# S5's B, C and tap matrices computed where they are used, from power tables transposed once

## The chip, the cores and the metric

One core of a Trainium2 chip runs the kernel. The metric is the device time of one execution in microseconds (us). TensorE is PE, VectorE DVE, ScalarE ACT, GpSimd POOL; SyncE (SP) issues all DMAs.

## The reference

Two layers, width 2048, over one sequence of 256 tokens. Each layer normalises x, multiplies it by one input matrix `w_in`, feeds the columns to four MoBA heads, four NSA heads and an S5 block (1024 channels in 64 groups of 16, each with 64 complex states), gates the three branches with SiLU and multiplies them by `w_out`. What the change touches is S5:

```python
mag = jnp.exp(dt * ar); ang = dt * ai
abar_r, abar_i = mag * jnp.cos(ang), mag * jnp.sin(ang)
nr, ni = abar_r - 1.0, abar_i
den = ar * ar + ai * ai
fr = (nr * ar + ni * ai) / den; fi = (ni * ar - nr * ai) / den
bbar_r = fr[..., None] * br - fi[..., None] * bim
bbar_i = fr[..., None] * bim + fi[..., None] * br
bu = einsum('bsgc,gpc->sbgp', ug, bbar)          # complex
x_t = abar * x_{t-1} + bu_t                      # associative scan
y = Re(einsum('sbgp,gcp->bsgc', x, c)) + d * u
```

## The kernel before, in words

**Projections.** Weights come in pieces of 512 KB: two rows of 128 inputs by 512 columns (`raw`). ACT rounds a piece to `whi`, DVE computes the remainder `wlo`; this pair is called a split here. Activations have the same two halves, `lhs`. PE then makes 12 products of 512 columns: `whi` with both halves and `wlo` with the high one. There are four buffers for `raw` and four for the halves of the weights. The columns of a layer come in chunks of 8 pieces, the first two (S5's inputs) together as 16 pieces named k=0 to 15 here; then the GLU and `wo`.

**S5.** `s5_setup` computes on [128, 64] tables the powers 0 to 4 of abar (`pwr`, `pwi`), f (`fr`, `fi`) and the phase `f4`. `s5_tables` loads B and C of half a layer (`bc`) and multiplies B by f in place. `s5_turns` lays scaled B out as `bpl` (ACT copies of 64 partitions) and makes the cosine and sine tables of the scan. A layer has 8 groups (`s5_group`), each with G=4 pairs of channel groups: `products` multiplies B by four powers (`PB`), PE transposes the four 128x128 blocks of `PB` into a PSUM bank, ACT copies the bank to `W1`; `products` multiplies C by three powers, ACT copies in power 0 and gathers all of it into `Cs`. Then PE forms the tap matrices from `Cs` and `bpl` (`w<-Cs,bpl`), multiplies, DVE scans, and PE multiplies the scan's result by C.

**Order.** Python generators (`Weave`) say after which weight piece a step may come, by the delays in `D`; the `Recorder` keeps every operation back, and `schedule` then lists them for all engines by priority, with estimated costs. PE's operations other than projection products are put into bursts between products; banks of PSUM are given out in order. `high_priority(offset)` moves an operation ahead by so many positions. All operations are issued on one line of a helper (L332, after the change L339), so tiles, not lines, tell them apart.

Of the kernel before, what the change touches and what calls it, by code (L numbers as in the profile page):

```python
# [29 lines left out]
G = 4  # L30
D = dict(sh=(1, 0), s0=(15, 21), s1=(4, 3), s2=(3, 5), s3=(1, 1), hn=(8, 4), hk=(4, 9), co=(8, 13), cg=(12, 5), cx=(3, 2), cp=(2, 2), at=(3, 8), pt=(2, 4), gap=(1, 2), ag=(3, 1), gt=(3, 4), lt=(1, 3), yt=(8, 4), gl=(0, 2), xt=(0, 45))
# [10 lines left out]
NEAR = 1  # L42
# [38 lines left out]
class Recorder:  # L81
# [24 lines left out]
    @staticmethod  # L106
    def box(ap):

        name = ap.tensor.name
        if name.startswith("in_") or name.startswith("out_"):  # L110
# [83 lines left out]
    def schedule(self):  # L194
# [67 lines left out]
        while left:  # L262
# [100 lines left out]
class Trunk:  # L363
# [62 lines left out]
    def load_consts(self):  # L426
        nc = self.nc
        t = self.cp.tile(list(self.a["cst"].shape), F, name="cst")
        nc.sync.dma_start(t, self.a["cst"])
        o = 0  # L430
        for nm, shape in cst_parts(self.L):
            n = math.prod(shape)
            v = t[:, o:o + n]
            if len(shape) > 1:
                v = v.rearrange(f"p ({' '.join('abc'[:len(shape)])}) -> p {' '.join('abc'[:len(shape)])}",
                                **dict(zip("abc", shape)))
            setattr(self, nm, v)
            o += n
        for nm, x in (("mask", self.mask), ("cmask", self.cmask), ("identb", self.ident)):
# [131 lines left out]
    def s5_setup(self):  # L571
# [5 lines left out]
        ar, ai, ld = self.a_re, self.a_im, self.logdt  # L577
# [25 lines left out]
        pr = self.cp.tile([128, n, 5], F, name="pwr")  # L603
        pi = self.cp.tile([128, n, 5], F, name="pwi")
        self.pr, self.pi = pr, pi
# [13 lines left out]
        self.rr = self.cp.tile([128, n, 4], F, name="pwrr")  # L619
        self.ri = self.cp.tile([128, n, 4], F, name="pwri")  # L620
        for q in range(4):
            nc.vector.tensor_copy(self.rr[:, :, q], pr[:, :, 4 - q])
            nc.vector.tensor_copy(self.ri[:, :, q], pi[:, :, 4 - q])
# [9 lines left out]
        self.fr = self.cp.tile([128, n], F, name="fr")  # L633
        self.fi = self.cp.tile([128, n], F, name="fi")
# [3 lines left out]
        tt(self.fr, t1, iv, OP.mult)  # L638
# [3 lines left out]
        tt(self.fi, t1, iv, OP.mult)  # L642
# [13 lines left out]
    def s5_tables(self, l, half):  # L656
        nc, sp, tt, ts = self.nc, self.sp, self.tt, self.ts
        n0 = 32 * l + 16 * half
        self.bc = sp.tile([128, 16, 4, 16], F, name="bc")
        nc.sync.dma_start(self.bc, self.a["bc"][l, :, 16 * half:16 * half + 16])  # L660
        br, bi = self.bc[:, :, 0], self.bc[:, :, 1]
        bb = lambda x: x[:, n0:n0 + 16, None].to_broadcast([128, 16, 16])
        t = [sp.tile([128, 16, 16], F, name=f"bt{j}", tag="g2", bufs=4) for j in range(4)]
        tt(t[0], br, bb(self.fr), OP.mult)
        tt(t[1], bi, bb(self.fi), OP.mult)
        tt(t[2], bi, bb(self.fr), OP.mult)
        tt(t[3], br, bb(self.fi), OP.mult)
        tt(br, t[0], t[1], OP.add)
        tt(bi, t[2], t[3], OP.subtract)

    def s5_turns(self, l, half):
        sp, tt = self.sp, self.tt
        n0 = 32 * l + 16 * half
        for h in range(2):
            q = slice(64 * h, 64 * h + 64)
            for r in range(2):
                self.act(self.bpl[64 * r:64 * r + 64, :, h, 16 * h:16 * h + 16], self.bc[q, :, r], AF.Copy)
# [11 lines left out]
    def s5_stream(self, l):  # L689

        if l == 0:
            yield from self.s5_setup()
# [5 lines left out]
        next(gens[0])  # L698
# [3 lines left out]
        for i in range(n + 2):  # L702
# [13 lines left out]
            if i < n:  # L716
                next(gens[i])
                if i + 1 < n:
                    if i + 1 == h:
                        self.s5_tables(l, 1)  # L720
                    next(gens[i + 1])
                if i % h == 0:
                    while not has(f"su{i // h}"):
                        yield 1
                next(gens[i])
                yield D["s1"][l] + (D["sh"][l] if i == h else 0)

    def s5_group(self, l, g):
# [4 lines left out]
        bc = self.bc[:, h0:h0 + G].rearrange("p a (t r) c -> p a t (r c)", t=2)  # L733

        def products(x, tr, ti, K, conj, first, **k):
            b = x[:, :, None, :].to_broadcast([128, G, K - first, 32])
            w = lambda v: v[:, n0:n0 + G, first:K, None].to_broadcast([128, G, K - first, 32])
            P = [sp.tile([128, G, K, 2, 16], F, **kw) for kw in (k, dict(name="P1", tag="g2", bufs=4))]
            for p, t in zip(P, (tr, ti)):
                tt(p[:, :, first:].rearrange("p a k r c -> p a k (r c)"), b, w(t), OP.mult)  # L740
            re, im = P[0][:, :, first:, 0], P[0][:, :, first:, 1]
            x0, x1 = (P[1][:, :, first:, q] for q in range(2))
            tt(re, re, x1, OP.add)
            tt(im, *((x0, im) if conj else (im, x0)), OP.subtract)
            return P[0]

        B = products(bc[:, :, 0], self.rr, self.ri, 4, False, 0, name="PB")
        yield
        W1 = sp.tile([128, G, 128], F, name="W1")
        pt = self.bank()  # L750
# [4 lines left out]
        for r in range(2):  # L755
            self.act(C[:, :, 0, r], bc[:, :, 1, 16 * r:16 * r + 16], AF.Copy, scale=1.0 - 2 * r)
        Cs = sp.tile([128, G, 2, 4, 16], F, name="Cs", bufs=2)
        for r in range(2):
            for e in range(2):
                self.act(Cs[64 * r:64 * r + 64, :, e], C[64 * e:64 * e + 64, :, :, r], AF.Copy)  # L760
# [607 lines left out]
    def run(self):  # L1368
        self.xd = self.dp.tile([128, 2, D_MODEL], F, name="xd")
        lhs = [None] * 16  # L1370
        with self.tc.high_priority(offset=40000):
# [8 lines left out]
            self.act(z, z, AF.Copy)  # L1380
        with self.tc.high_priority(offset=19000):
            self.nc.sync.dma_start(self.nw, self.a["nw"])
            self.load_consts()
# [38 lines left out]
def cst_parts(L):  # L1422
    return [("a_re", [L * 32]), ("a_im", [L * 32]), ("logdt", [L * 32]), ("dcol", [L, 32 // G]), ("jt", [64]),
            ("eye32", [32]), ("ident", [128]), ("ropec", [2, 32]), ("ropes", [2, 2, 16]), ("ropekc", [32]),
            ("ropeks", [2, 16]), ("valid", [2]), ("sel", [16]), ("mask", [128]), ("cmask", [2, 128]), ("mri", [2])]


def layout(inputs):
# [26 lines left out]
    d["a_re"], d["a_im"] = st(i["s5_a_re"]), st(i["s5_a_im"])  # L1455
    d["logdt"] = st(np.repeat(i["s5_log_dt"][:, :, None], 64, 2))
    b = lambda x: x.reshape(L, 32, 2, 64, 16).transpose(0, 2, 3, 1, 4).reshape(L, 128, 32, 16)
    g = lambda x: x.reshape(L, 32, 2, 16, 64).transpose(0, 2, 4, 1, 3).reshape(L, 128, 32, 16)
    d["bc"] = c(np.stack([b(i["s5_b_re"]), b(i["s5_b_im"]), g(i["s5_c_re"]), g(i["s5_c_im"])], 3))
# [20 lines left out]
```

## Time and profile before

| | |
|---|---|
| time, median of 3 runs | 869.31 us (869.24 to 869.38) |
| the profiled execution | 869.47 us |
| its span on the core | 867.7 us |
| busy: PE, PE weight load, DVE, ACT | 861.3, 710.0, 657.9, 568.4 us |
| bytes moved by DMA | 167.95 MB, 194 GB/s |
| TensorE clock granted | full in all 40 slices |

Busy time of an engine is the time in which an operation of it was under way. Operations of PE overlap in their records, so the step from one start to the next is what a product costs, and the recorded duration is longer.

### The profile page before, as it was taken

The page shows a single profiled execution, that of the slowest core. Times are in us where ns is not written, and L with a number is a line of the kernel's source. Part 1 is how long each engine was busy: PE and PEld are TensorE (multiplying, and loading weights), DVE is VectorE, ACT ScalarE, POOL GpSimd, SP SyncE. Part 2 cuts the span into 40 slices and gives each one's busy share as a digit, 9 for nine tenths or more (in the row PEclk, how much of TensorE's full clock was granted, in tenths as well). Part 3 has the DMA queues.
Part 4 walks back from the last instruction along what each step waited for, and adds up shares of the span by engine and source line. Part 5 has one row for each costly group of instructions (what it writes and reads, how often), then busy time and mean ns, then how long its engine had stood idle before and what let it go on. Part 6 is the DMA issues. An engine that isn't in the chain of part 4 may idle for free.

```text
span 867.7 us, 14290 instructions
## 1 busy us (share of the span) xinstructions
PE 861.3 (99%) x5107; PEld 710.0 (82%) x5107; DVE 657.9 (76%) x1381; ACT 568.4 (66%) x1084; POOL 10.3 (1%) x50
## 2 busy tenths in 40 slices
PE   9999999999999999999999999999999999999998
PEld 6888987877788888888888888888878888888886
DVE  6789999989868568755666899998996654675552
ACT  6588767687887866544645665697788575554331
POOL 1000000000000000000000000000000000000000
PEclk9999999999999999999999999999999999999999
DMA  9897486645524557677764666756552645665772
GB/s 310 279 297 232 132 282 208 205 126 178 157 65 138 184 170 243 194 243 242 225 213 132 197 215 205 252 176 194 168 171 74 205 130 161 188 191 182 242 242 97
DMA packets 66103, 167.95 MB, mean 194 GB/s; under 512 B 13424, under 2 KB 22128, under 8 KB 66032
## 3 DMA queue, kind: packets, MB, share of 16 engines
q1 hardware_dynamic: 66032, 167.04, 61.0%
q8 instruction: 40, 0.66, 0.3%
q14 instruction: 31, 0.25, 0.1%
HBM read 161.77 MB, written 5.24 MB: 192 GB/s over the span
## 4 chain that ended last, share of the span: by engine, by line
PE 84%; DVE 11%; DMA 2%; issue 1%; ACT 1%; SPq 0%; DVEq 0%; ACTq 0%
PE acc L332 72%; PE w L332 9%; DVE wlo L332 3%; PE o L332 3%; DVE t L332 1%; DMA raw<-in_w_a 1%; DVE Z L332 1%; DVE P L332 1%; ACT whi L332 1%; DVE q L332 1%; DMA raw<-in_w_p 1%; DVE z L332 1%; DVE qn L332 1%; DVE PB L332 0%; DVE XP L332 0%
## 5 line engine op out<-in xcount | busy, mean ns | idle before, releaser
L332 PE MATMUL acc<-whi,lhs 128*128 128x512 f32 (+1 forms) x2176 | 667.1, 386 | 0.1
L332 PEld LDWEIGHTS acc<-whi,lhs 128*128 128x128 f32 x2176 | 403.4, 188 | 82.2 <-issue 2.4
L332 DVE TENSOR_TENSOR wlo<-raw,whi 128x1024 fp32r<-128x1024 f32 (+2 forms) x275 | 323.7, 1179 | 163.7 <-ACT whi L332 162.7
L332 PE MATMUL acc<-wlo,lhs 128*128 128x512 f32 (+1 forms) x1088 | 418.0, 384 | 0.0
L332 ACT ACTIVATE whi<-raw 128x1024 fp32r<-128x1024 f32 (+2 forms) x275 | 281.5, 1026 | 191.5 <-PE acc L332 131.1
L332 PEld LDWEIGHTS acc<-wlo,lhs 128*128 128x128 f32 x1088 | 204.6, 188 | 40.4 <-issue 1.0
L332 ACT ACTIVATE P<-w,sst,hrs 128x128 f32<-128x128 f32 (+2 forms) x64 | 29.7, 477 | 8.0 <-DVE sst L332 7.7
L332 ACT ACTIVATE Cs<-P 64x256 f32<-64x256 f32 x64 | 26.5, 414 | 5.8 <-DVE P L332 2.6
L332 DVE TENSOR_TENSOR Z<-q,q 64x252 f32<-64x252 f32 x64 | 26.5, 414 | 0.9
L332 ACT ACTIVATE Uz<-Ud,cst 128x512 f32<-128x512 f32 x32 | 22.8, 719 | 4.5 <-DVE hrs_t L332 1.9
L332 ACT ACTIVATE sq<-acc,rstd 128x128 f32<-128x128 f32 x56 | 20.6, 368 | 5.0 <-DVE qn L332 4.1
L332 ACT ACT_TABLE_LOAD x14 | 18.0, 1283 | 3.0 <-DVE sst L332 2.1
L332 DVE TENSOR_TENSOR_SCAN z<-dec,t 128x512 f32<-128x512 f32 x16 | 19.3, 1206 | 0.1
L332 ACT ACTIVATE dec<-m 128x256 f32<-128x256 f32 x32 | 12.2, 410 | 8.7 <-DVE z L332 8.2
L332 PE MATMUL w<-Uz,W 128*64 128x128 f32 x256 | 17.5, 279 | 0.0
L332 DVE TENSOR_REDUCE sst<-w 128x2 f32<-128x512 f32 (+2 forms) x22 | 12.9, 599 | 5.2 <-PE w L332 5.2
L332 DVE TENSOR_TENSOR xc<-acc,xc 128x512 f32<-128x512 f32 x16 | 10.3, 683 | 7.9 <-PE acc L332 7.9
L332 DVE TENSOR_TENSOR lhs<-w,lhs 128x256 fp32r<-128x256 f32 x32 | 12.2, 416 | 4.5 <-ACT lhs L332 3.2
L332 PEld LDWEIGHTS w<-Uz,W 128*64 128x64 f32 x256 | 13.6, 136 | 1.5
L332 DVE SCALAR_TENSOR_TENSOR zs<-zt,zs 128x512 f32<-128x512 f32 x16 | 10.8, 686 | 4.0 <-ACT zs L332 4.0
L332 ACT ACTIVATE zt<-acc,rstd 128x512 f32<-128x512 f32 x16 | 11.0, 685 | 4.2 <-PE acc L332 4.0
L332 DVE STREAM_TRANSPOSE Ud<-su 128x256 f32<-128x256 f32 x32 | 13.6, 429 | 0.0
(234 smaller groups left out, 791.9 us busy)
## 6 DMA issues: line engine op xcount, KB each, us to landing
raw<-in_w_a SPq DMA_DIRECT2D x160, 512.0 KB, 4.5
raw<-in_wo SPq DMA_DIRECT2D x64, 512.0 KB, 4.7
craw<-in_cw SPq DMA_DIRECT2D x32, 256.0 KB, 3.6
raw<-in_glu SPq DMA_DIRECT2D x16, 512.0 KB, 4.2
raw<-in_w_p SPq DMA_DIRECT2D x15, 512.0 KB, 5.2
raw<-in_w_b SPq DMA_DIRECT2D x16, 268.0 KB, 4.0
xs<-in_x SPq DMA_DIRECT2D x8, 256.0 KB, 5.6
bc<-in_bc SPq DMA_DIRECT2D x4, 512.0 KB, 5.8
```

The costliest lines, as they stand in the source:

```text
L332: o.fn(*o.args, **o.kw)
```

## The change: what it does

`s5_setup` gets its three inputs (`sm`) in a DMA of their own behind k=2 and runs with a high priority from the beginning of the kernel. It ends with products of f and the powers (`tx`), four transposes of `tx` on PE, two ACT copies and eight DMAs to a DRAM table `tw`, and with sixteen ACT copies of 64 partitions into the tables `tc` and `tf`. Per group, `W1` is two loaded tables times two loaded copies of B (tables `T` read from `tw`, each row to 16 partitions; `B` laid out by the host): three operations of 512 columns on DVE, no transpose, no ACT copy. `Cs` is likewise three operations on DVE from `cc`, which the host lays out, and `tc`. `bpl` is two products and two sums on DVE. The smaller constants move: the masks have their own DMA, the rest comes later. The scheduler lets no more than four accumulator banks be out, and two delays in `D` change.

```diff
@@ schedule
+                    if tag["share"] and tag["first"] and tag["held"] == 4:
+                        return None
@@ s5_setup, at its end
+        X = self.kp.tile([128, 2, L, 4, 32], F, name="tx", tag="t2", bufs=T2)
+        for q in range(4):
+            for w, (x, y, op) in enumerate(((pr, pi, OP.subtract), (pi, pr, OP.add))):
+                tt(t1, fr, x[:, :, 4 - q], OP.mult)
+                tt(t2, fi, y[:, :, 4 - q], OP.mult)
+                tt(X[:, w, :, q], pair(t1), pair(t2), op)
...
+                nc.tensor.transpose(pv[:, w, l], X[:, w, l].rearrange("p q a -> p (q a)"), self.ident)
+        self.act(xs, pv, AF.Copy)
+        self.act(xn, pv[:, 1], AF.Copy, scale=-1.0)
...
+                    nc.sync.dma_start(self.tw[l][:, r, w], x[:, l])
@@ s5_turns
-                self.act(self.bpl[64 * r:64 * r + 64, :, h, 16 * h:16 * h + 16], self.bc[q, :, r], AF.Copy)
+                self.nc.sync.dma_start(b[j], self.a["bb"][l, :, half, j])
+            tt(b[j], b[j], self.tf[j][:, n0:n0 + 16, :, None].to_broadcast([128, 16, 2, 16]), OP.mult)
+        for e in range(2):
+            tt(self.bpl[:, :, e, 16 * e:16 * e + 16], b[0][:, :, e], b[1][:, :, e], OP.add)
@@ s5_group
-        B = products(bc[:, :, 0], self.rr, self.ri, 4, False, 0, name="PB")
-        for i in range(G):
-            nc.tensor.transpose(pt[:, 128 * i:128 * i + 128], B[:, i].rearrange("p s r c -> p (s r c)"), self.ident)
-        self.act(W1.rearrange("p a n -> p (a n)"), pt, AF.Copy)
-        C = products(bc[:, :, 1], self.pr[:, :, :4], self.pi[:, :, :4], 4, True, 1, name="P0", tag="g2", bufs=4)
-                self.act(Cs[64 * r:64 * r + 64, :, e], C[64 * e:64 * e + 64, :, :, r], AF.Copy)
+        for w in range(2):
+            T, B = (sp.tile([128, G * 128], F, name=f"{x}{w}", tag="tb", bufs=2) for x in "TB")
+            with self.tc.high_priority(offset=TB):
+                nc.sync.dma_start(T, bass.AP(tensor=tw.tensor, offset=tw.offset + 4096 * w + 128 * p0,
+                                             ap=[[8192, 8], [0, 16], [1, G * 128]]))
+                nc.sync.dma_start(B, self.a["bt"][l, :, w, 128 * p0:128 * (p0 + G)])
+            tt(T if w else Wf, T, B, OP.mult)
+        tt(Wf, Wf, T, OP.add)
+        for j, o in enumerate((Cs, P1)):
...
+            tt(v(o), c[:, :, None, :].to_broadcast([128, 2 * G, 4, 16]), t[:, :, :, None].to_broadcast([128, 2 * G, 4, 16]),
...
+        tt(f(Cs), f(Cs), f(P1), OP.add)
```

What the lists of the engines show of it, at three places. On DVE, the splits of k=1, 2 and 3 at the start; before:

```order
L332 TENSOR_TENSOR wlo<-raw,whi 128x512 x2
L332 SCALAR_TENSOR_TENSOR lhs<-xt,lhs 128x256 x2
L332 TENSOR_TENSOR wlo<-raw,whi 128x512 x2
L332 TENSOR_TENSOR wlo<-raw,whi 128x1024
L332 SCALAR_TENSOR_TENSOR lhs<-xt,lhs 128x256 x2
```

and after the change (`et` are setup's values; the first comes from `sm`):

```order
L339 TENSOR_TENSOR wlo<-raw,whi 128x512 x2
L339 SCALAR_TENSOR_TENSOR lhs<-xt,lhs 128x256 x2
L339 TENSOR_SCALAR et_99<-sm 128x64
L339 TENSOR_SCALAR et_99<-et_99 128x64
L339 TENSOR_TENSOR wlo<-raw,whi 128x512 x2
L339 TENSOR_SCALAR et_99<-et_99 128x64
L339 SCALAR_TENSOR_TENSOR et_99<-et_99 128x64
L339 TENSOR_SCALAR et_99<-et_99 128x64
L339 SCALAR_TENSOR_TENSOR et_99<-et_99 128x64
L339 TENSOR_SCALAR et_99<-et_99 128x64
L339 SCALAR_TENSOR_TENSOR et_99<-et_99 128x64 x2
L339 TENSOR_TENSOR wlo<-raw,whi 128x1024
```

Setup's small operations now stand ahead of the early splits, nine of them ahead of that of k=3.

On PE, a burst that held nothing but one group's transposes, in the midst of a chunk, before:

```order
L332 MATMUL acc<-wlo,lhs 128x512
L332 MATMUL w<-cst,PB 128x128 x4
L332 MATMUL acc<-whi,lhs 128x512 x2
L332 MATMUL acc<-wlo,lhs 128x512
L332 MATMUL acc<-whi,lhs 128x512 x2
```

There are 16 such sets of four, in bursts of their own or with others; now there is one set, of `tx`, early in layer 0:

```order
L339 MATMUL acc<-wlo,lhs 128x512
L339 MATMUL w<-cst,tx 128x128 x4
L339 MATMUL acc<-whi,lhs 128x512 x2
L339 MATMUL acc<-wlo,lhs 128x512
L339 MATMUL acc<-whi,lhs 128x512 x2
```

On PE, the end of layer 0's attention (`mkT`, `mqT` scores, `P` transposes, `PT` products), after the change, between the last products of the last chunk (`mz`):

```order
L339 MATMUL w<-cst,P 128x128 x4
L339 MATMUL w<-mkT,mqT 128x256
L339 LDWEIGHTS identb
L339 MATMUL w<-mask,identb 128x128
L339 MATMUL w<-mkT,mqT 128x256
L339 LDWEIGHTS identb
L339 MATMUL w<-mask,identb 128x128
L339 MATMUL w<-cst,P 128x128 x4
L339 MATMUL o<-vs,PT 128x128 x2
L339 MATMUL o<-vw,PT 128x128 x2
L339 MATMUL w<-cst,P 128x128 x4
L339 MATMUL acc<-wlo,lhs 128x512
```

Before, the scores of `mkT` began 13 weight pieces ahead of that place, and such steps stood in several bursts with products between them; now they stand in two.

## Rows read from the trace of the kernel before

**Rows 1.** The page: busy time, share and instructions of each engine.

```profile
PE 861.3 (99%) x5107; PEld 710.0 (82%) x5107; DVE 657.9 (76%) x1381; ACT 568.4 (66%) x1084; POOL 10.3 (1%) x50
```

**Rows 2.** The page: the chain that ended last, by engine.

```profile
PE 84%; DVE 11%; DMA 2%; issue 1%; ACT 1%; SPq 0%; DVEq 0%; ACTq 0%
```

**Rows 3.** Waits of PE after its start: tile, releaser, us in total, times, longest.

```profile
PE w L332 <- DVE P L332: 1.0, 1, 1.0
PE w L332 <- ACT Cs L332: 0.3, 1, 0.3
```

**Rows 4.** Windows: us, busy and (instructions) by engine, PE clock, DMA share, GB/s.

```profile
20.00:36.00 16.00, 16.00 (x73) 13.23 (x72) 11.03 (x15) 10.07 (x17) 0.00 (x0) 1.00 0.95 341
36.00:47.00 11.00, 11.00 (x50) 9.13 (x49) 8.63 (x34) 4.91 (x6) 0.00 (x0) 1.00 0.66 185
130.00:175.00 45.00, 45.00 (x350) 35.85 (x349) 44.79 (x134) 30.99 (x71) 0.45 (x4) 1.00 0.67 204
```

**Rows 5.** PE's timeline around one group's transposes: start, us, operation.

```profile
86.49 0.39 PE L332 MATMUL acc<-wlo,lhs 128*128 128x512 f32 x1
86.72 0.60 PE L332 MATMUL w<-cst,PB 128*128 128x128 f32 x4
87.08 0.48 PE L332 MATMUL acc<-whi,lhs 128*128 128x512 f32 x1
```

**Rows 6.** The same for a group that shares its burst.

```profile
224.76 0.60 PE L332 MATMUL w<-cst,PB 128*128 128x128 f32 x4
225.20 0.59 PE L332 MATMUL o<-vblk,PTc 128*128 128x512 f32 x1
```

**Rows 7.** Instruction groups by form: count, busy us, mean ns, idle before.

```profile
L332 ACT ACTIVATE Cs<-P 64x256 f32<-64x256 f32 x64 | 26.5, 414 | 5.8 <-DVE P L332 2.6 <-DVE hrs_i L332 1.1 <-DVE hrs_y L332 1.0
...
L332 DVE TENSOR_TENSOR PB<-PB,P 128x256 f32<-128x256 f32 x32 | 13.2, 414 | 0.0
L332 DVE TENSOR_TENSOR PB<-bc,pwrr 128x512 f32<-128x512 f32 x16 | 10.9, 678 | 0.0
...
L332 PE MATMUL w<-cst,PB 128*128 128x128 f32 x64 | 9.9, 277 | 0.0
```

**Rows 8.** DVE's timeline, small operations among splits.

```profile
37.50 0.48 DVE L332 SCALAR_TENSOR_TENSOR lhs<-xt,lhs 128x256 fp32r<-128x256 f32 x1
37.90 1.26 DVE L332 SCALAR_TENSOR_TENSOR et<-et 128x64 f32<-128x64 f32 x5
...
39.44 0.22 DVE L332 TENSOR_TENSOR pr<-pr,cst 128x64 f32<-128x64 f32 x1
39.59 1.22 DVE L332 TENSOR_TENSOR wlo<-raw,whi 128x1024 fp32r<-128x1024 f32 x1
40.72 0.21 DVE L332 TENSOR_TENSOR pr<-pr,cst 128x64 f32<-128x64 f32 x1
```

**Rows 9.** DVE's timeline, split of k=3; PE's, first `wlo` products of k=4, k=15.

```profile
12.58 1.23 DVE L332 TENSOR_TENSOR wlo<-raw,whi 128x1024 fp32r<-128x1024 f32 x1 [0.42 <-ACT whi L332]
...
17.81 0.39 PE L332 MATMUL acc<-wlo,lhs 128*128 128x512 f32 x1
...
45.69 0.39 PE L332 MATMUL acc<-wlo,lhs 128*128 128x512 f32 x1
```

**Rows 10.** ACT's timeline: softmax steps of an attention; a table load.

```profile
237.88 0.55 ACT L332 ACTIVATE P<-w,sst,hrs 128x256 f32<-128x256 f32 x1
...
238.42 0.55 ACT L332 ACTIVATE P<-w,sst,hrs 128x256 f32<-128x256 f32 x1
...
240.96 0.50 ACT L332 ACTIVATE P<-P,co 128x256 f32<-128x256 f32 x1
241.37 0.35 ACT L332 ACTIVATE sq<-acc,rstd 128x128 f32<-128x128 f32 x1
...
49.95 1.28 ACT L332 ACT_TABLE_LOAD   x1
```

**Rows 11.** The page, DMA issues: count, KB each, median us to landing.

```profile
craw<-in_cw SPq DMA_DIRECT2D x32, 256.0 KB, 3.6
```

More of the change, by code (lines that the diff above doesn't have):

```diff
@@ L41 @@
 MARGIN, MERGE, AHEAD = 2000, 300, 4
-NEAR = 1
+NEAR, TB, SETUP = 1, 19000, 19500
 class Weave:
@@ L438, in load_consts @@
             o += n
-        for nm, x in (("mask", self.mask), ("cmask", self.cmask), ("identb", self.ident)):
+        ms = self.sp.tile([128, 3, 128], F, name="ms", tag="Uz")
+        nc.sync.dma_start(ms, self.a["msk"])
+        for nm, x in (("mask", ms[:, 0]), ("cmask", ms[:, 1:]), ("identb", self.ident)):
             m = self.cp.tile(list(x.shape), BF, name=nm)
@@ L576, in s5_setup @@
         tt, ts, stt = self.tt, self.ts, self.stt
-        ar, ai, ld = self.a_re, self.a_im, self.logdt
+        sm = self.sm
+        ar, ai, ld = (sm[:, q] for q in range(3))
         self.exp(dt, ld, [128, n], "0")
@@ L618, in s5_setup @@
         yield
[L619 to L623, printed above, removed]
         self.m4 = self.cp.tile([128, n], F, name="m4")
@@ L632, in s5_setup @@
         nc.vector.reciprocal(iv, den)
-        self.fr = self.cp.tile([128, n], F, name="fr")
-        self.fi = self.cp.tile([128, n], F, name="fi")
+        fr, fi = m, cs
         tt(t1, nr, ar, OP.mult)
@@ L641, in s5_setup @@
         tt(t1, t1, t2, OP.add)
-        tt(self.fi, t1, iv, OP.mult)
+        tt(fi, t1, iv, OP.mult)
+        yield
+        X = self.kp.tile([128, 2, L, 4, 32], F, name="tx", tag="t2", bufs=T2)
+        pair = lambda x: x.rearrange("p (l a) -> p l a", l=L)
+        for q in range(4):
[3 more added lines that the diff above has]
+                tt(X[:, w, :, q], pair(t1), pair(t2), op)
+        self.ct = [self.cp.tile([128, n, 2, 4], F, name=f"tc{j}") for j in range(2)]
+        self.tf = [self.cp.tile([128, n, 2], F, name=f"tf{j}") for j in range(2)]
+        for e in range(2):
+            q = slice(64 * e, 64 * e + 64)
+            for j, (x, y, sgn) in enumerate(((pr, pi, 1.0), (pi, pr, -1.0))):
+                self.act(self.ct[j][:64, :, e], x[q, :, :4], AF.Copy)
+                self.act(self.ct[j][64:, :, e], y[q, :, :4], AF.Copy, scale=sgn)
+            for j, (x, y, sgn) in enumerate(((fr, fi, -1.0), (fi, fr, 1.0))):
+                self.act(self.tf[j][:64, :, e], x[q], AF.Copy)
+                self.act(self.tf[j][64:, :, e], y[q], AF.Copy, scale=sgn)
+        p = self.bank()
+        pv = p.rearrange("p (w l n) -> p w l n", w=2, l=L)
+        for w in range(2):
+            for l in range(L):
+                nc.tensor.transpose(pv[:, w, l], X[:, w, l].rearrange("p q a -> p (q a)"), self.ident)
+        xs = self.kp.tile([128, 2, L, 128], F, name="tp0", tag="t2", bufs=T2)
+        xn = self.kp.tile([128, L, 128], F, name="tn0", tag="t2", bufs=T2)
+        self.act(xs, pv, AF.Copy)
+        self.act(xn, pv[:, 1], AF.Copy, scale=-1.0)
+        self.tw = [self.dp.tile([4, 2, 2, 32, 128], F, name=f"tw{l}") for l in range(L)]
+        for l in range(L):
+            for r, w, x in ((0, 0, xs[:, 0]), (0, 1, xs[:, 1]), (1, 0, xn), (1, 1, xs[:, 0])):
+                with self.tc.high_priority(offset=20000 if l == 0 else 0):
+                    nc.sync.dma_start(self.tw[l][:, r, w], x[:, l])
         yield
@@ L656, in s5_tables @@
     def s5_tables(self, l, half):
[L657 to L669, printed above, removed]
+        nc, sp = self.nc, self.sp
+        self.cc = sp.tile([128, 2, 16, 2, 16], F, name="cc")
+        with self.tc.high_priority(offset=20000 if l else 18900):
+            nc.sync.dma_start(self.cc, self.a["cc"][l, :, half])
     def s5_turns(self, l, half):
@@ L673, in s5_turns @@
         n0 = 32 * l + 16 * half
-        for h in range(2):
-            q = slice(64 * h, 64 * h + 64)
-            for r in range(2):
-                self.act(self.bpl[64 * r:64 * r + 64, :, h, 16 * h:16 * h + 16], self.bc[q, :, r], AF.Copy)
+        b = [sp.tile([128, 16, 2, 16], F, name=f"bb{j}", tag="g2", bufs=4) for j in range(2)]
+        for j in range(2):
+            with self.tc.high_priority(offset=20000 if l else 18900):
+                self.nc.sync.dma_start(b[j], self.a["bb"][l, :, half, j])
+            tt(b[j], b[j], self.tf[j][:, n0:n0 + 16, :, None].to_broadcast([128, 16, 2, 16]), OP.mult)
+        for e in range(2):
+            tt(self.bpl[:, :, e, 16 * e:16 * e + 16], b[0][:, :, e], b[1][:, :, e], OP.add)
         self.cos = sp.tile([128, 16, 64], F, name="cosT")
@@ L691, in s5_stream @@
         if l == 0:
-            yield from self.s5_setup()
+            setup = self.s5_setup()
+            while True:
+                with self.tc.high_priority(offset=SETUP):
+                    if next(setup, 1):
+                        break
+                yield
         n = 32 // G
@@ L697, in s5_stream @@
         gens = [self.s5_group(l, g) for g in range(n)]
-        next(gens[0])
         yield 1
@@ L732, in s5_group @@
         h0 = p0 % 16
[L733 to L745, printed above, removed]
@@ L757, in s5_group @@
-        Cs = sp.tile([128, G, 2, 4, 16], F, name="Cs", bufs=2)
-        for r in range(2):
-            for e in range(2):
-                self.act(Cs[64 * r:64 * r + 64, :, e], C[64 * e:64 * e + 64, :, :, r], AF.Copy)
+        W1 = sp.tile([128, G, 128], F, name="W1")
+        tw, Wf = self.tw[l], W1.rearrange("p a n -> p (a n)")
+        for w in range(2):
+            T, B = (sp.tile([128, G * 128], F, name=f"{x}{w}", tag="tb", bufs=2) for x in "TB")
[4 more added lines that the diff above has]
+            tt(T if w else Wf, T, B, OP.mult)
@@ L1380, in run @@
             self.act(z, z, AF.Copy)
+        with self.tc.high_priority(offset=19900):
+            self.sm = self.kp.tile([128, 3, self.L * 32], F, name="sm", tag="t2", bufs=T2)
+            self.nc.sync.dma_start(self.sm, self.a["sm"])
         with self.tc.high_priority(offset=19000):
@@ L1454, in layout @@
     st = lambda x: c(x.reshape(L, 32, 2, 64).transpose(2, 3, 0, 1).reshape(128, L * 32))
[L1455 to L1459, printed above, removed]
+    d["sm"] = c(np.stack([st(i["s5_a_re"]), st(i["s5_a_im"]), st(np.repeat(i["s5_log_dt"][:, :, None], 64, 2))], 1))
+    b, g = (np.stack([i[f"s5_{n}_re"], i[f"s5_{n}_im"]]) for n in "bc")
+    b = b.reshape(2, L, 2, 16, 2, 64, 16)
+    d["bb"] = c(np.tile(b.transpose(1, 5, 2, 0, 3, 4, 6), (1, 2, 1, 1, 1, 1, 1)))
+    d["cc"] = c(np.tile(g.reshape(2, L, 2, 16, 2, 16, 64).transpose(1, 6, 2, 0, 3, 4, 5), (1, 2, 1, 1, 1, 1, 1)))
+    d["bt"] = c(np.tile(b.transpose(1, 6, 0, 2, 3, 4, 5).reshape(L, 16, 2, 32 * 128), (1, 8, 1, 1)))
+    d["msk"] = c(np.concatenate([d.pop("mask")[:, None], d.pop("cmask")], 1))
     d["dcol"] = c(i["s5_d"].reshape(L, 32 // G, G * 32).transpose(2, 0, 1))
```

31 lines of the change are left out of this document (18 added, 13 removed).

## The prediction

> **What bounds the kernel now.** I read the busy shares first: PE 99%, DVE 76%, ACT 66% of the span [rows 1]. A busy PE can still be a slow one, so next the chain that ended last: PE 84% and DVE 11% [rows 2]; DVE is on it with splits, but a chain only says who came last before each step, not by how much. Hence the waits of PE: after its start there are two, 1.0 and 0.3 us, both in S5 or attention beside it [rows 3]. In windows of the first half PE is busy without a gap while DVE is at 44.79 of 45 us [rows 4]: DVE is full there and PE is still fed. The granted clock is full in each of these windows [rows 4]. So PE's own work sets the time: a step from product to product takes 86.72 - 86.49 = 0.23 us [rows 5], with nothing between. What PE is relieved of comes off the span, as long as ACT and DVE keep ahead of it; what ACT is relieved of comes off only where PE would wait for it.
>
> **The change part by part.**
>
> *PE.* 64 transposes go, 16 sets of four. A set in the midst of products takes 87.08 - 86.72 = 0.36 us [rows 5]; one in a burst with other steps 225.20 - 224.76 = 0.44 [rows 6]. 16 sets: 5.8 to 7.0 us. Their recorded durations, which overlap, give 9.9 [rows 7], an upper end. Most sets stand in shared bursts, so I take 6.8. Four transposes of `tx` come, 0.4 by the same rows. Net -6.4 (-5.4 to -9.5).
>
> The set shown pushed the next product back by 0.36, between products at steps of 0.23 [rows 5]: it lay in no bubble. The Trainium skill, "Perfetto Trace Analysis", section "Identifying the Most-Contended Engine", says that the busy share of matmuls is a poor measure of how near TensorE is to its limit, and that the busy share of weight loads should be read: by that, 82% [rows 1], there would be headroom, the sets could lie in it, and the term would be 0. What it would do here is a rival below.
>
> *DVE, per group.* Out go two products of 512 columns at 0.68 and two sums at 0.41 for `PB` [rows 7], and as many for C with three quarters of the columns: between 3.3 (at three quarters) and 4.4. In come six operations of 512 columns at 0.68: 4.1 [rows 7]. That is within 0.8 of even, either way; over 16 groups -5 to +13 us of 658, and spread out. Setup brings 24 small operations more, 0.15 to 0.25 each [rows 8], some 5 us. None of that is on the path by itself: in rows 4 DVE is full for 45 us and PE doesn't wait, and four halves of splits, each worth 12 products or 2.7 us of PE, lie between them. I take 0 for it.
>
> *DVE, early.* What matters is where setup's operations go: ahead of the splits of k=3 to 15, by the order lists. Before, the split of k=3 ended at 12.58 + 1.23 = 13.8 and PE wanted that of k=4 at 17.81 [rows 9]. Small operations cost 0.25 in a chain (1.26 for five), 0.15 where independent, an `lhs` 0.40, a split 1.13 to the next operation [rows 8]. Ahead of k=3 nine small ones come, 1.4 to 2.2 us; before them, DVE also waits for `sm`, which lands behind k=2. DVE had idle time there (0.42 ahead of the split [rows 9]), so k=3 ends at 14 to 15.7; then two `lhs` (0.8), four chained ones (1.0) and the split of k=4: 17.0 to 18.7 against 17.81. From there to the split of k=15 the list has 58 small operations, ten `lhs`, ten splits and one of 1024 columns: 58 x 0.20 + 10 x 0.40 + 11 x 1.13 = 28.0, so the last split starts at 17.8 + 28.0 = 45.8 and ends at 47.0; PE's product with it is at 45.69 [rows 9]. With 0.15 each it ends at 44.1, in time; with 0.25 at 49.9, 4.2 late. DVE was idle for 5.0 of 16 and 2.4 of 11 us there [rows 4], which is what setup fills. I take +1.0, bounds 0 and +4.2, as most of the operations in the lists are chains of two or three, in between. Once PE has waited there, nothing gives it back, since PE has no slack later. After that DVE has less to do than before ahead of the same splits, as setup is done.
>
> *ACT.* It loses 64 copies for `Cs`, 26.5 us [rows 7], the 32 for power 0, 16 for `W1` and 16 for `bpl`; it gets 16 for `tc` and `tf`, two for `tx`, and four table loads at 1.28 [rows 10], since setup's exponentials and sines now fall between other functions. ACT isn't what PE waits for but in one row of 0.3 us [rows 3], so its relief is worth that, and it is counted below.
>
> *The end of layer 0.* Here the order moves work together. The last scores, softmaxes and products of attention stood over 13 weight pieces; now PE has them in two bursts. What ACT must do within them is, by its list, some 32 operations of 128 to 512 columns at 0.41 to 0.54 (the steps from 240.96 to 241.37 and from 237.88 to 238.42 [rows 10]), 15.0 at 0.47; five of 1024 columns at 1.0, 5.0; two table loads, 2.6 [rows 10]: 22.6 us. PE's own steps in that stretch are worth some 58 of 0.23, 13.2. So PE would stand for 9.4 us if both came to it together. But in the stretch ahead of it ACT has 15.5 us of work where PE has 22.7, so it can be 7.2 ahead. PE then waits 9.4 - 7.2 = 2.2; bounds 0 (the lead is larger since ACT is relieved everywhere) and 9.4 (no lead, because ACT waits for PE's scores). I take 2.2, nearer to the lead's end, for PE's products between these bursts come later than ACT's inputs.
>
> *Waits that go.* The 1.0 and 0.3 [rows 3] had `P` from a loaded DVE and `Cs` from ACT copies; both are relieved: -1.3 (0 to -1.3).
>
> *DMA.* 32 loads of `T` and 32 of `B`, 256 KB each, and eight for `bpl`: 18.9 MB on 168, spread over both layers, where the queues are at 0.66 and 0.67 in two windows and 0.95 only in 20 to 36 us [rows 4]. Such a load lands 3.6 us after its issue [rows 11]. The two buffers make the loads of a group's second half wait until DVE has used the first, so DVE, with the splits queued behind, may stand for up to 3.6 us less what is between; the splits in store (8 us of PE) hide it: 0, bounds 0 and +3. SP has 82 more issues; it is 0% of the chain [rows 2]. The masks and the smaller constants move behind the first weights, where nothing needs them: 0. The wait of `tx`'s transposes for DVE and the first `T`, two transfers later: 0 to +1, I take 0, as the first group comes well behind.
>
> *Sum.* -6.4 + 1.0 + 2.2 - 1.3 = -4.5. The profiled execution took 869.47 (span 867.7); 865.0, and as it was 0.16 above the median of the runs, **864.8** against 869.31.
>
> **The rivals.**
>
> *The end of layer 0 eats it (slower).* If ACT has no lead, PE stands 9.4 us there: -6.4 + 1.0 + 9.4 - 1.3 = +2.7, 872.0. It decides from a lead below 1.0 us on, where the whole passes 0.2%, or 1.74 us, about what a measurement of this kernel can tell from no change. For it: softmax needs PE's scores, which stand in the same bursts. Against: ACT loses over 40 us elsewhere. 0.11.
>
> *Setup holds up the first splits.* At 0.25 for each small operation PE is 4.2 late: -6.4 + 4.2 + 2.2 - 1.3 = -1.3, 868.0. For it: chains at 0.25 [rows 8]. Against: the list isn't all chains. 0.13.
>
> *The transposes were in bubbles.* If PE had gaps that its records hide, the 64 are worth 0, and then 0.4 + 1.0 + 2.2 - 1.3 = +2.3, 871.6. Against it are the steps of product to product [rows 5]. 0.04.
>
> *ACT and DVE keep ahead everywhere.* No wait early and none at the end of layer 0: -6.4 - 1.3 = -7.7, 861.6. For it: PE waits only 1.3 us in all before [rows 3], with a full DVE. Against: the sums above. 0.17.
>
> **How the numbers follow.** The forecast has 0.55, with a range of its own from 863 to 867. Faster by over 0.2% (under 867.6): 0.53 of the forecast, the whole 0.17, 0.03 of the early wait: 0.73. Within 0.2%: 0.02 of the forecast, 0.10 of the early wait, 0.02 and 0.01 of the rivals that end near 872: 0.15. Slower (over 871.0): 0.09 + 0.03 = 0.12. The range reaches from 860.8, below the case of no waits by the 9.9 us of rows 7, to 870.0, which takes in the early wait with +2 for loads; it leaves out the slow rivals (0.15) and little below.
>
> **What would show it.** In the profile of the changed kernel: no transposes of `PB`, steps of product to product unchanged at 0.23, so PE's work without waits 6 us shorter; in the waits of PE a row for `wlo` on DVE before 50 us, of 0 to 4 us; a row for `P` or `PT` on ACT at the end of layer 0 between the last products of `mz`, of about 2; none for `W1` or `Cs` beyond some tenths. If PE's waits come to over 5 us, the forecast is wrong, and their tile names the step; if they come to under 1, the last rival holds. Waits for `T` or `B` on DVE are expected and cost nothing, unless a wait of PE for a split follows.

## The result, and the profile after

The changed kernel takes 879.88 us (median of 4 runs, 879.8 to 880.5) against 869.27: ratio 1.0123, interval 1.0106 to 1.0141, some 10.6 us slower. The profiled execution took 880.5 us, its span 878.6. The page's busy shares and chain, as in [rows 1, 2]:

```profile
PE 861.6 (98%) x5047; PEld 703.7 (80%) x5047; DVE 664.3 (76%) x1357; ACT 534.5 (61%) x978; POOL 10.2 (1%) x50
...
PE 60%; DVE 16%; DMA 13%; ACT 5%; issue 4%; SPq 1%; ACTq 0%; DVEq 0%
```

60 instructions fewer on PE and 106 on ACT, as the change says, but the chain now runs 13% of the time over DMAs, where it was 2%. The waits of PE, as in [rows 3] (two then, 1.3 us; the third row here is the one at the start):

```profile
PE acc L339 <- DVE wlo L339: 3.5, 6, 0.9
PE w L339 <- DMA tp<-pkd: 1.9, 2, 1.2
PE w L339 <- DVE hpi L339: 1.2, 1, 1.2
PE o L339 <- DVE XP L339: 0.9, 1, 0.9
PE w L339 <- ACT Y L339: 0.9, 1, 0.9
PE w L339 <- ACT P L339: 0.7, 1, 0.7
PE w L339 <- DVE P L339: 0.7, 1, 0.7
PE w L339 <- ACT PT L339: 0.5, 1, 0.5
```

Seven more rows of 0.2 to 0.5 us follow; without the one at the start all come to 11.7 us. They name many tiles on three engines, so no single consumer is the cause; look at what feeds them. ACT's waits for weight pieces of `in_w_a`, before (first row) and after, and DVE's waits for the new loads:

```profile
ACT whi L332 <- DMA raw<-in_w_a: 12.1, 10, 3.2
```

```profile
ACT whi L339 <- DMA raw<-in_w_a: 78.4, 46, 5.4
...
DVE T L339 <- DMA B<-in_bt: 9.0, 5, 3.9
DVE W L339 <- DMA B<-in_bt: 4.8, 1, 4.8
```

Windows as in [rows 4], and one more, in which DVE was busy 19.71 of 20 us before:

```profile
20.00:36.00 16.00, 16.00 (x73) 13.23 (x72) 15.80 (x53) 12.04 (x19) 0.00 (x0) 1.00 0.88 282
36.00:47.00 11.00, 11.00 (x50) 9.13 (x49) 10.83 (x26) 8.59 (x17) 0.00 (x0) 1.00 0.81 274
66.00:86.00 20.00, 20.00 (x92) 16.40 (x90) 8.02 (x10) 7.87 (x13) 0.00 (x0) 1.00 0.76 247
130.00:175.00 45.00, 43.12 (x270) 33.93 (x269) 42.20 (x115) 22.22 (x45) 1.21 (x4) 1.00 0.80 255
```

Setup fills DVE early and PE isn't held (16.00 and 11.00). Then, from 66 to 86 us, DVE stands for 12 us: 4.8 of them for the `T` and `B` of S5's first group, the rest for `whi`, which is no loss by itself (in e1 below, which loses nothing, DVE is busy 10.84 of these 20 us). The chain of waits there, columns start and us:

```profile
71.74 3.99 DMA tw<-tn
75.81 0.64 SPq L339
76.50 0.45 SPq L339
77.00 0.42 SPq L339
77.52 9.29 DMA raw<-in_w_a
```

SP stands 2.4 us at the first `T` until the write of `tw` has landed; the second piece behind it is issued at 77.52 and takes 9.29 us where 4.5 is the median before. Later SP stands at the head of its queue for the new loads to land, and all that is queued behind stands with it: 33.3 us in the change (the two rows), 11.8 us in e1 below, of which the third row is most:

```profile
SPq L339 <- DMA B<-in_bt: 21.4, 12, 4.6
SPq L339 <- DMA T<-tw: 11.9, 8, 2.4
...
SPq L776 <- DMA B<-in_bt: 9.3, 4, 4.6
```

Where the time goes is read from PE's projection products, 12 a piece, by the start of the first one after so many pieces; the table has the difference to the kernel before (us), one execution each, and when the first `T` was issued. At the eighth piece, ahead of S5's first group, the rows stand at -0.2 to +1.1 already, one execution differing from another (e1 +0.1, the change +0.7, the change again +1.0, and +0.9 in the last row, which has changed nothing up to there). The changed order has other steps of PE ahead of a mark than the order before (2.3 us less work up to piece 48), so what a load costs up to a mark is read against e1, which has the same order:

```
                            first T   48 pieces  112 pieces  the end   48 to end
change                         75.8      +3.4       +9.2      +10.5      +7.1
change again (c1)              76.8      +2.6       +7.7      +10.0      +7.4
T from input (e1)              72.9      +0.2       +1.0       -0.9      -1.1
narrow loads (e2)              76.1      +0.6       +1.3       -0.6      -1.2
128 rows of tw (e6)            77.0      +1.6       +2.0       +0.4      -1.2
8 rows of input (e7)           73.4      +1.5       +2.9       +1.4      -0.1
mostly 8 rows of input (e9)    75.6      +2.1       +5.0       +4.8      +2.7
two copies by SP               79.8      +8.0       +9.9       +8.0       0.0
four copies by SP              85.7     +19.3      +19.9      +18.0      -1.3
second copy later (b2)         76.9     +10.3      +11.5       +9.8      -0.5
W1 as before (f4)                -       -0.7       +0.8       +2.2      +2.9
before less 48 transposes        -       +0.9       +0.1       -2.5      -3.4
```

### The profile page after: what moved, and what is told of

It reads as the page before. It is cut to its first block, busy times and chain, and to the rows that moved or that the text cites. A ratio compares the mean times of both kernels' runs of the same rounds, so it can differ in the third digit from the quotient of the medians.

```text
span 878.6 us, 14159 instructions
## 1 busy us (share of the span) xinstructions
PE 861.6 (98%) x5047; PEld 703.7 (80%) x5047; DVE 664.3 (76%) x1357; ACT 534.5 (61%) x978; POOL 10.2 (1%) x50
## 2 busy tenths in 40 slices
DMA packets 77559, 187.35 MB, mean 213 GB/s; under 512 B 14384, under 2 KB 24496, under 8 KB 77488
## 4 chain that ended last, share of the span: by engine, by line
PE 60%; DVE 16%; DMA 13%; ACT 5%; issue 4%; SPq 1%; ACTq 0%; DVEq 0%
PE acc L339 53%; DMA raw<-in_w_a 7%; PE w L339 5%; DVE wlo L339 5%; ACT whi L339 2%; PE o L339 2%; DVE t L339 2%; DMA B<-in_bt 1%; SPq L339 1%; DVE z L339 1%; DVE Z L339 1%; DMA cc<-in_cc 1%; DVE q L339 1%; DVE W L339 1%; DMA tp<-pkd 1%
## 5 line engine op out<-in xcount | busy, mean ns | idle before, releaser
L339 DVE TENSOR_TENSOR wlo<-raw,whi 128x1024 fp32r<-128x1024 f32 (+2 forms) x275 | 323.2, 1178 | 147.3 <-ACT whi L339 146.1
L339 ACT ACTIVATE P<-w,sst,hrs 128x128 f32<-128x128 f32 (+2 forms) x64 | 29.7, 479 | 11.9 <-DVE sst L339 11.8
L339 DVE TENSOR_TENSOR_SCAN z<-dec,t 128x512 f32<-128x512 f32 x16 | 19.3, 1205 | 0.0
L339 DVE TENSOR_REDUCE sst<-w 128x2 f32<-128x512 f32 (+2 forms) x22 | 12.9, 599 | 7.5 <-PE w L339 7.4
L339 DVE TENSOR_TENSOR xc<-acc,xc 128x512 f32<-128x512 f32 x16 | 10.4, 684 | 10.0 <-PE acc L339 10.0
L339 DVE TENSOR_TENSOR T<-T,B 128x512 f32<-128x512 f32 x16 | 11.0, 687 | 9.1 <-DMA B<-in_bt 9.0
L339 PE MATMUL w<-tp,U 128*64 128x128 f32 x128 | 13.3, 285 | 1.9 <-DMA tp<-pkd 1.9
L339 DVE TENSOR_TENSOR W<-T,B 128x512 f32<-128x512 f32 x16 | 10.9, 682 | 4.8 <-DMA B<-in_bt 4.8
L339 PE MATMUL w<-Cs,Z 128*64 128x64 f32 x256 | 13.2, 222 | 0.5 <-DVE Z L339 0.5
```

Of the source, the lines that this page charges most:

```text
L339: o.fn(*o.args, **o.kw)
```

## The experiments

Except where W1 is built otherwise or the planner is edited, an experiment keeps the order of instructions on PE, DVE and ACT word for word: the planner plans the change, and only the DMA that is issued differs. So a difference between two of these runs comes from the transfers. (In e2 and e3 the products read their 64 columns eight times.)

**T from elsewhere, fewer bytes, another queue.** The edits, at the load of `T` (and `B`):

```diff
-nc.sync.dma_start(T, <8 rows of tw, each to 16 partitions>)
+e1: nc.sync.dma_start(T, a["bt"][l, :, w, 128 * p0:128 * (p0 + G)])
+e2: nc.sync.dma_start(T[:, :64], <the same 8 rows of tw, 64 columns>); B[:, :64] likewise
+e3: both
+e4: nc.gpsimd.dma_start(...) for T and B as they are
```

> The changed kernel in its own order of instructions on all engines, but each T is read from an input of the same size instead of the DRAM table tw, so no load waits for the writes of tw (W1 is then wrong: T is not the power table). Theory A, the round trip through DRAM: the first T stands about 4 us at the head of SP's queue, raw pieces behind it come late, DVE idles from 70 to 86 us and is behind afterwards: the 4.3 us of waits for wlo at 86 to 117 us go, some of the later ones too, 870 to 875. Theory B, bytes: 16.8 MB of T and B more make every piece late: no change, 878.5 to 880. Theory C, order: DVE's list simply has S5's work too late whatever the loads do: no change, 879 to 880.

> The changed kernel in its own order, but each load of T and B brings 64 of the 512 columns, which the products read eight times (W1 is then wrong); the wait of T for the writes of tw stays. 14.7 MB less are moved. Theory A: the wait at the head of SP's queue stays, so 876 to 880. Theory B: the pieces come as before the change, 866 to 871. Theory C: 879 to 880.

> Both edits at once, same order: T from an input, and 64 of 512 columns of T and B. Theories A and B both expect the waits for loads to be gone, 864 to 870; if A alone is right it equals e1, if B alone it equals e2. Theory C: 879 to 880 still, as the order is the same; whatever is left above 863 (the time before less the transposes) is what the order costs.

> The changed kernel, result and bytes the same, same order on PE, DVE and ACT, but the loads of T and B are issued on GpSimd's DMA queue instead of SP's, so that what they wait for (tw, the ring of two buffers) no longer stands ahead of raw pieces, pkd and tp. Theory A in its wider form (waits at the head of SP's queue): ACT's 78 us of waits for raw fall to near the 12 of before, PE's waits with them, 868 to 874. Theory B: the bytes are there all the same, 878 to 881. Theory C: 879 to 880.

Against the kernel before (869.52): e1 869.39 us, ratio 1.0001 (0.9992 to 1.001); e2 868.85, 0.9995; e3 869.36, 0.9996; e4 884.18, 1.0174 (1.0157 to 1.0191). Theory C falls: with the same order the loads alone cost 10.5 us. B as stated falls too: e1 moves all the bytes (187.34 MB) and loses nothing by them. A as stated falls with e2, which keeps the wait for `tw`. What e1 and e2 share is that no full-size load reads `tw`. ACT's waits for `in_w_a` fall to 46.4 in e1 (not to the 12.1 of before, which shows how little idle time of ACT says), and PE's waits lose all that came from DMAs:

```profile
PE acc L343 <- DVE wlo L343: 2.1, 4, 0.8
PE w L343 <- DVE hpi L343: 1.2, 1, 1.2
PE acc L343 <- DVE lhs L343: 0.6, 1, 0.6
PE w L343 <- ACT PT L343: 0.5, 1, 0.5
PE w L343 <- DVE Z L343: 0.5, 1, 0.5
```

e4 does relieve ACT (46.5 us of waits for `in_w_a`), and yet DVE waits 17.9 us for `T` and `B`: another queue frees the pieces, not the loads.

**Wait or pattern.** e6 reads 128 different rows of `tw` (`ap=[[512, 128], [1, 512]]`), e7 reads 8 rows of an input, each to 16 partitions; e9 takes 64 columns from `tw` and 448 from an input, both as 8 rows for 16.

> The changed kernel in its own order; each T still waits for the writes of tw and still brings 256 KB of tw, but as 128 different rows of 2 KB instead of 8 rows that 16 partitions each read (W1 is then wrong). Theory D, the repeated read: 16 readers of the same few rows of DRAM make the load slow and hold the queues for all others: 868 to 871, as with T from an input. Theory A and B together (the wait only hurts when the full bytes follow it): wait and bytes are both there, 878 to 881.

> The changed kernel in its own order; T comes from an input, with no wait for tw, but in the same pattern as the change reads tw: 8 rows of 2 KB, each to 16 partitions (W1 is then wrong). Theory D: the repeated read is slow wherever it reads, 877 to 881. Theory A and B together: no wait, so 868 to 871.

> The changed kernel itself, on this chip beside the others: 1.011 to 1.013 of the kernel before, 879 to 881. If it were below 873, the earlier comparisons with T from an input would have to be read against another chip.

> The changed kernel in its own order; of each T 64 columns come from tw, with the wait for its writes, and 448 from an input in the same pattern of 8 repeated rows (W1 is then wrong; 32 more DMAs). Theory E, sum and slack: the wait and the repeated read each make the first W1 about 2 us late, which the splits in store hide, and only both together run them out: 877 to 882. Theory F: reading the table tw itself in that pattern is what costs, wherever the wait is: 870 to 873.

e6 870.86, ratio 1.0013 (1.0004 to 1.0023); e7 871.37, 1.0022 (1.0011 to 1.0033), both against 869.6; c1 880.2, 1.0126 (1.0109 to 1.0143); e9 875.33, 1.0061 (1.0046 to 1.0076), against 870.17. By the medians, neither the wait with another pattern (e6) nor the pattern on an input (e7) costs over 2 us. e9 fits neither of its theories: with the wait, the pattern on an input and an eighth of each `T` from the table it loses 5.2 us, more than e6 and e7 together. What the pattern on the table costs by itself shows behind piece 48, where no load waits for `tw` any more: 7.1 to 7.4 us in the change, -0.1 in e7, -1.2 in e6. (e9 loses 2.7 there, by its small part of the table or by its 32 further loads; no run parts these.) It is visible in the four microseconds from the issue of one and the same `T` on (in S5 of layer 0; columns as in [rows 4], the last three are clock, DMA share, GB/s). In the change again, in e7, in e6, in e1, and in the run with two copies by SP (below), one row each:

```profile
243.40:247.40 4.00, 4.00 (x19) 3.33 (x18) 4.00 (x8) 0.86 (x1) 0.00 (x0) 1.00 0.47 72
```

```profile
239.80:243.80 4.00, 4.00 (x19) 3.30 (x19) 4.00 (x8) 1.06 (x1) 0.00 (x0) 1.00 0.50 137
```

```profile
239.40:243.40 4.00, 4.00 (x20) 3.30 (x19) 4.00 (x8) 1.06 (x1) 0.00 (x0) 1.00 0.68 234
```

```profile
237.90:241.90 4.00, 4.00 (x19) 3.32 (x18) 4.00 (x9) 1.06 (x1) 0.00 (x0) 1.00 0.75 245
```

```profile
246.20:250.20 4.00, 4.00 (x19) 3.34 (x18) 4.00 (x8) 1.06 (x1) 0.00 (x0) 1.00 0.52 152
```

After this `T` in the change the queues move 72 GB/s at half their share, with pieces issued behind it waiting; with different rows they move 234 and 245. This load is one of the slowest: over the same four microseconds of all 32 the means are 183 GB/s in the change again, 204 in e7, 258 in e6, 260 in e1, 209 with two copies. What the late loads do to the rest is better read from SP's waits for `T` and `B` to land: 34.2 us in the change again, 25.3 in e7, 16.9 with two copies, 14.2 in e6, 11.8 in e1. The chain of the change again shows it at the load above, with PE's wait that ends it:

```profile
243.40 5.87 DMA T<-tw
249.28 6.62 DMA tp<-pkd
...
256.04 0.44 PE L339 MATMUL w<-tp,U 128*64 128x128 f32 x4 [0.92 <-DMA tp<-pkd]
```

**Copies of the table.** `tw` is written two or four times, and each copy serves 8 or 4 partitions a row; the load's access becomes `[[4096, 16], [0, 8], [1, 512]]` with two. First the further copies went by GpSimd's queue, then all by SP's, and last SP wrote layer 0's second copy only behind the first loads of `T` and `B` and two pieces.

> The change with its power table written to DRAM twice (the second copy by GpSimd's queue), so that each row is read by 8 partitions instead of 16; result, bytes read and the order of instructions the same. If many reads of one row are what slows the queues: between the change (880) and T from an input (869), 873 to 878. If the table in DRAM costs for another reason (the wait for its writes, where it lies): no change, 879 to 882.

> The same with four copies, three of them by GpSimd's queue: each row is read by 4 partitions; the first T may wait some 3 us longer for the writes. If many reads of one row are the cause: below the two copies, 870 to 875. Otherwise 879 to 883.

> The two copies of the power table as before, but both written by SyncE's queue (GpSimd's queue had issued its writes 3.2 us apart, so that the first T came 10 us late): 4 writes more ahead of the first T, some 2 us. Each row is read by 8 partitions. If many reads of one row are the cause: 872 to 877. If not: 880 to 884.

> Four copies, all written by SyncE's queue: 12 writes of 0.53 us more ahead of the first T, so it and the pieces behind it are some 6 us later, which may cost up to 4 once; each row is read by 4 partitions. If many reads of one row are the cause, the rest comes near T from an input: 870 to 875. If not: 882 to 888.

> The change with two copies of the power table, the second copy of layer 0 written only behind the first loads of T and B and the two pieces after them, so that the first T is no later than in the change (76 to 77 us); the first T is read by 16 partitions a row, all later ones by 8; result and order of PE, DVE and ACT the same. If the cost is the sum of the first T's lateness and of the readers of a row, the first 48 pieces go as in the change (+1 to +3 against the kernel before) and the rest as with two copies (0): 869.5 to 873. If the two only act together in some other way, 876 to 880.

Totals: 881.87 (ratio 1.014) and 914.31 (1.0519) with GpSimd's queue; 877.86 (1.0095, 1.008 to 1.011) and 887.69 (1.021) with SP's; 879.01 (1.0105) for the last, against 869.64 to 869.97. By totals none of the five came out where many reads of one row as the cause had put it: 881.87, 887.69 and 879.01 lie in the range of the other theory, the other two in neither. The table by pieces says why, for each copy costs on the way to the first group, and parts the two. **Behind piece 48** the loss of 7.1 to 7.4 us is gone, 0.0 and -1.3 (GpSimd's: +0.2 and -1.2; the last: -0.5), which is where T from an input stands (-1.1). **Up to piece 48** the loss grows with how late SP gets on: with a first `T` at 76.8, 79.8 and 85.7 us the kernel stands 2.6, 8.0 and 19.3 behind. In the last run the first `T` was in time (76.9) and it stands 10.3 behind all the same: its four writes stood ahead of the next pieces, and the second `T` was issued at 92.6 instead of 87.0. A part of these losses is the clock, which stayed at full in the change: with two copies by SP the granted clock was 0.83 from 115 to 125 us; with four 0.86, 0.85 and 0.87 in 85 to 95, 115 to 125 and 125 to 140 us; in the last run 0.83, 0.78 and 0.92 in 95 to 105, 115 to 125 and 125 to 140 us. By these figures it took up to 1.7, 5 and 5 us (an estimate).

The round trip through DRAM alone costs little in the change. The runs that keep the wait of the first `T` without its slow load, e2 (first `T` at 76.1 us) and e6 (77.0), stand at +0.6 and +1.6 at piece 48, and +0.6 and +0.8 of that was there at the eighth piece. What further lateness costs, the copies show.

**The rest of the change.** Three questions: what transposes are worth in the kernel before (three of each four not issued); what the rest of the change does when W1 is built as before; and with it, the planner's two rules undone, or setup later. And one attempt to mend: the planner told that `T` and `B` land 5 us later.

```diff
 # before less 48 transposes
+if i: <not issued>
 # W1 as before (f4); g2: also without the limit of four banks, cx=(3, 2), cp=(2, 2); g1: also sm behind 20 more DMAs
+tt(p, x, t[:, n0:n0 + G, :, None], OP.mult) ...; nc.tensor.transpose(...); self.act(W1, pt, AF.Copy)
 # f7, in schedule
+o.end = dma + 800 + LATE.get(name, 0)     # T, B: 5000; tw: 2500
```

> The kernel before in its own order, but of the four transposes of a group only the first is issued, and the copy to W1 reads that block four times (W1 is then wrong). 48 of 64 transposes less. If PE's term of the prediction holds (0.09 to 0.11 us a transpose, nothing hidden): 4.3 to 5.2 us less than the kernel before, 864 to 865.2. If the transposes lay in bubbles: 869, no change.

> One part of the change undone: W1 comes from products, four transposes on PE and an ACT copy, as before the change; Cs, bpl, the early setup and the planner's rules stay as changed (no tw, no T, no B; one buffer less for temporaries). If the loads of T and B cost the 10.5 us and the 64 transposes are worth 3 to 6: 869 to 873. If the rest of the change is the harm: 875 to 880. If it is a gain by itself, since ACT has 36 us less: 863 to 868.

> W1 as before the change (as in the run that undid that part, 1.0039 of the kernel before), and the planner's limit of four banks and the two delays also as before. If those rules are what the rest of the change loses by: 868 to 870.5. If they help: 874 to 880.

> W1 as before the change, the planner's rules as changed, but the inputs of S5's setup are loaded 20 DMAs later, so that setup starts behind the split of k=15 instead of among the first ones. If the early setup costs by standing ahead of splits: 869 to 872. If setup now delays the first groups: 873 to 880.

> The change, with one edit to the planner: it takes loads of T and B as landing 5 us later, and writes of tw 2.5 us later, than its estimate, so that the products for W1 stand further back in DVE's list (result the same). If DVE's wait at the head of its queue, with splits behind it, is what turns late loads into waits of PE, most of it goes: 866 to 873. If the late pieces themselves hold PE, or DVE is simply full afterwards: 876 to 882.

Less 48 transposes: 866.78, ratio 0.9962 (0.9949 to 0.9975), so 2.2 to 4.4 us of the 4.3 to 5.2 expected. By pieces, from the eighth on (where this execution stood at +0.9), layer 0's 24 gave 0.8 us and layer 1's gave 2.6, what 24 by 0.107 come to. Followed step by step, each of layer 0's eight sets gave its 0.32 us at its place, too. But 1.0 us was lost again between 110 and 133 us, where PE's products need `wlo` and `XP` from DVE, and 0.7 at 187 us, where PE waits for `kn`. From 102 to 142 us DVE is busy 39.93 of 40 us in the kernel before:

```profile
102.00:142.00 40.00, 40.00 (x374) 32.65 (x373) 39.93 (x122) 26.48 (x55) 1.21 (x4) 1.00 0.75 242
```

W1 as before: 873.1, 1.0039 (1.0024 to 1.0054): the rest of the change loses some 3 us, too, though this run also has one buffer less for temporaries, and no run parts the two. It isn't the planner's rules (g2 872.88, 1.0041), and setup among the first splits helps (g1, later: 878.05, 1.0096, with 4.9 us of PE's waits for `PB`). f7 missed widely: 903.75, 1.0391; S5 and attention were put off, and PE waited 12.9 us for `P`, with a granted clock of 0.57 in 114 to 126 us. Only the run without 48 transposes beats the kernel before by more than the noise, and it leaves work out.

## Why the prediction was wrong, step by step

- **The step that failed is the DMA term**, "0, bounds 0 and +3", for loads of `T` that I priced by `craw`'s 3.6 us [rows 11]. That row reads 128 different rows; `T` reads 8 rows 16 times over, and the one in the chain above took 5.87. It cost some 10.5 us (880 against 869.4 in e1): at piece 48 the change stands 2.4 to 3.2 us behind e1 (0.6 to 0.9 of it from the eighth piece already), and after that piece it loses 8.2 to 8.5 more. The wait for `tw`, which the term also put at 0, is little by itself (e2, e6). I also wrote that the queued splits would hide what DVE waits. They nearly do so for the first wait (after DVE's 4.8 us PE is held 0.9 us, up to 87.51), but the term left out that SP's queue passes a late load on: SP stood 33.3 us for `T` and `B` to land, and the pieces behind came late.
- A rule would have warned of a part of it. The Trainium skill, "DMA: Bandwidth & Descriptors", section "Rules for kernel authors", states that a DMA is spread over engines by the slowest dimension of its access patterns, and that an outermost dimension below 16 confines it to at most that many engines; `T`'s source has 8. The trace agrees by its count of packets: the change and e7 have 14,384 packets under 512 B, e1 and e6 14,640: eight more for each of the 32 loads, as if each engine that takes part added one. The share after such a load, 0.47 and 0.50, is no sign of it, for with two copies and an outer dimension of 16 it is 0.52. The rule isn't the whole: e7 has the same 8 and loses 1.8 us, and two copies change the outer dimension and the readers of a row at once. Which of the two it is on the table, and why the table is worse than an input, the runs leave open.
- **PE's term**, -6.4: the work did go. Taking each of PE's steps at the usual length of its kind (the median), the sum falls by 5.8 us. What failed is "what PE is relieved of comes off the span": of transposes left out of the kernel before, layer 0 kept less than a third. "DVE is full there and PE is still fed" was read from 130 to 175 us, and after 133 us nothing was lost again there; but from 102 us on DVE, busy 39.93 of 40 us, was level with PE, and what PE was relieved of turned into waits. The rival with transposes in bubbles falls, for each set gave its 0.32 us at its place in both layers.
- **Early DVE**, +1.0: right that it bears setup (15.80 and 10.83 us busy), wrong that PE waits: from 9 to 60 us no PE wait is listed. The small operations came faster than 0.20 each: the split of k=15 ended at 46.0 (44.79 and 1.22), where the sum had 47.0. The first products with `wlo` of k=4 and k=15 start at 18.37 and 46.37, 0.56 and 0.68 after [rows 9], nearly all of it from one wait of 0.51 us for `whi` at 8.86.
- **End of layer 0**, 2.2: two bursts (314.5 to 323.2 and 325.1 to 330.8 us), as the list had it, but no wait of PE is listed in either; `PT`'s 0.5 us stands ahead of them, at 297 us. **Waits that go**, -1.3: `P`'s wait for DVE is 0.7 where it was 1.0, and that for `Cs` is gone; in e1 both are gone.
- The sum as it came: -5.8 of work, +12.7 of longer waits (steps over 0.15 us beyond the usual: 3.0 us before, 15.7 in the change, 6.9 in e1), +3.5 of small ones, 10.4 at PE's last product (10.5 by the table). For e1: -5.8 + 3.9 + 1.0 = -0.9. So without the DMA term's error the kernel would stand at 869.4, still 4.6 us above the forecast. That these last waits come from the order, or from the work moved to DVE, is not shown: e1, e2 and e3 have both in common, with different transfers, and agree within 0.6 us, but g2, which undid two of the planner's rules with W1 as before, changed nothing.
- Of the signs named beforehand, waits of PE over 5 us came (11.7); that their tile would name the step did not, as they spread over many tiles. The lower end of the range, 860.8, isn't what its reason gives: with 9.9 us for the transposes it would be 869.3 - 9.5 - 1.3 = 858.5. It bore on nothing.
- Slower had been given 0.12, by the end of layer 0 or by bubbles. It came by neither.

## What to carry to other kernels

Price a load by a row with the same access pattern, not only the same size: readers per row and the outer dimension belong to the price. Before such a load goes onto the queue that feeds the bounding engine, ask what stands behind it there, and read that queue's own waits: here they ranked the change, e7 and e1 (34.2, 25.3 and 11.8 us) where ACT's waits did not tell e7 from e1 (49.9 and 46.4). When a second engine is full for 40 us, a microsecond taken off the first is worth what the second lets through; leaving work out of the old kernel, at the old order, measures that in one run.

## What the runs showed of the hardware that was not expected

GpSimd's DMA queue issued writes of 64 KB some 3.2 us apart in layer 0, though each took 0.69 us of it (in the run with four copies by it):

```profile
82.82 0.69 POOL L687 DMA_DIRECT2D t2w<-tp  x1 [2.53 <-issue]
86.13 0.69 POOL L687 DMA_DIRECT2D t2w<-tp  x1 [2.62 <-issue]
89.00 0.69 POOL L687 DMA_DIRECT2D t2w<-tp  x1 [2.18 <-issue]
```

SP's queue issued twelve of the same in 7.44 us (four copies by SP). And a wait of PE can cost twice: in e4, PE had been idle for 1.1 of the four microseconds from 275 us on, then stood 2.63 us for attention's `P` up to 282.38 us. In the window of that wait (279 to 283 us) the granted clock was 0.82, behind it 0.50 (1.2 of 2.4 GHz) for five microseconds:

```profile
275.00:279.00 4.00, 2.90 (x53) 2.50 (x55) 2.99 (x5) 1.47 (x2) 0.24 (x2) 1.00 0.21 64
279.00:283.00 4.00, 1.36 (x26) 1.12 (x26) 3.10 (x5) 3.99 (x14) 0.00 (x0) 0.82 0.75 230
283.00:288.00 5.00, 5.00 (x24) 3.65 (x16) 4.90 (x15) 4.35 (x17) 0.00 (x0) 0.50 0.05 18
288.00:292.00 4.00, 4.00 (x20) 3.22 (x19) 3.43 (x7) 2.36 (x5) 0.00 (x0) 0.95 0.22 57
```

Products there were 0.43 us apart instead of 0.23. In the change itself the clock stayed at full.
